# Matmul, GELU, matmul on one core: turns of `a` in halves, earlier casting loads, another order of sums, and tiles moved to multiples of 512 bytes

## Chip, core and metric

The kernel runs on one core of a Trainium2 chip. The metric is the device time of that core in microseconds, as a median of several runs.

## The reference

```python
m, k, n, p = 1024, 1024, 2048, 1024
h = a @ b                                  # a: 1024x1024, b: 1024x2048, float32
h = 0.5 * h * (1 + tanh(sqrt(2/pi) * (h + 0.044715 * h**3)))
out = h @ c                                # c: 2048x1024, float32
```

## The kernel before

The order of the work is written out by hand: every engine runs its instructions in the order in which the Python text issues them, and the tiles wait for each other through semaphores. Slots in SBUF and banks in PSUM are named by hand too (`slot`, `bank`, `pieces`), and allocated one after the other along a partition.

**Front.** `a` comes in eight loads of 512 KB (`load_a(h, q)`: half `h` of the rows, quarter `q` of the columns), and the first quarter of the columns of `b` in four (`load_b(q)`), all on SP's queue in the order a(0,0), b(0), a(1,0), then a(0,q), b(q), a(1,q) for q = 1, 2, 3. They land as float32. `cast_a` casts one load of `a` to bfloat16 on VectorE or ScalarE; `turn` transposes it on TensorE with eight 128x128 transposes into one PSUM bank, and two VectorE copies bring it to `aT`. `cast_b` casts `b` on ScalarE. `block(h, tiles, ks)` then issues matmuls of the first 512 columns of `b` against `aT`, for half `h` of the rows of `a`: 64 matmuls of 128x128 by 512 in all, four output tiles per half. Since only seven banks are free beside the bank of the turns, the fourth tile of half 1 is made last (`mm1(ps[1, 3], ...)`, in bank 7), and the last turn, a(1,3), goes through bank 0 once `gelu` has read it. The rest of `b` and all of `c` come by casting loads on POOL's queue (1 MB read, 512 KB of bfloat16 written, each). POOL's queue holds them back with one small copy, `gate` (L82), that reads the last load but two, a(0,3), and so waits for it.

**Small round, `seven(zero, ...)`.** `seven` computes a 2x2 block product with seven block products in place of eight. Its products are called P1 (A11 by B11), P2 (A12 by B21), P5, P6, P7 (products of sums), and then `p4` and `p3`. The sums `s1` to `s4` and `t1` to `t4` are made on VectorE (`dve`, L152) in the type fp32r; P1 and P2 multiply bfloat16 tiles, the other five multiply fp32r tiles. `snap` (L278) copies a product from PSUM to SBUF on ScalarE, `plus` (L283) adds it to another product on VectorE. In the round `zero` (256 columns of `b`), each product has 2 output tiles with 4 matmuls each: 56 matmuls. Its sums `s` need the casting loads of `b`.

**Middle round, `seven(one, ...)`,** does the same for the last 1024 columns of `b`: 7 products, 4 tiles, 4 matmuls each, 112 matmuls. Every output tile of both rounds goes through GELU on ScalarE into `hT`.

**Last round, `seven(two, ...)`,** is the second matmul, `hT` by `c`: 7 products, 4 tiles, 8 matmuls each, 224 matmuls with a last P2 tile kept for the very end in two halves (L349). Its results go through `ot` buffers (four of them, tag `o`) to SP's stores.

All matmuls of `seven` are issued at one line, L194. In the program as it is built, the wide tiles `c_sb`, `hT`, `aT`, `b1`, `b2`, the four slots `x0` to `x3` and all `pieces` start 448 bytes above a multiple of 512 bytes in the partition: the small tiles ahead of them end at byte 17,856 = 34 x 512 + 448, and the wide tiles all have sizes that are multiples of 512.

Of the kernel before, what the change touches and what calls it, by code (L numbers as in the profile page):

```python
# [9 lines left out]
F32 = mybir.dt.float32  # L10
# [9 lines left out]
def kernel(ctx, tc, a, b, c, out):  # L20
    nc = tc.nc
    M, K = a.shape
    _, N = b.shape
    _, P = c.shape
    H = 512
# [8 lines left out]
    consts = ctx.enter_context(tc.tile_pool(name="consts", bufs=1))  # L34
# [8 lines left out]
    def bank(i, shape=(128, H), dt=F32, name="ps"):  # L43
        return pp.tile(list(shape), dt, name=name, tag=f"bank{i}", padded_shape=None)

    def pieces(tag, bufs, shape, dt, name):
        return small.tile(shape, dt, name=name, tag=tag, bufs=bufs)
# [5 lines left out]
    gate = consts.tile([128, 1], F32, name="gate")  # L53
    g = consts.tile([128, 1], F32, name="g")

    c_sb = keep.tile([128, NT, P], BF16, name="c_sb")
    hT = [keep.tile([128, NT, H], BF16, name=f"hT{h}") for h in range(2)]
    aT = slot("a", [128, 2, KT, H], BF16, "aT")
# [6 lines left out]
    sta = [slot(f"x{i}", [128, 2, 2, 4, 256], F32, "sta") for i in (1, 3)]  # L65

    def load_a(h, q):
        nc.sync.dma_start(out=sta[q // 2][:, h, q % 2],  # L68
                          in_=av[:, 4 * h:4 * h + 4, ds(q * 256, 256)])

    def load_b(q):
        nc.sync.dma_start(out=stb[:, 2 * q:2 * q + 2], in_=bv[:, 2 * q:2 * q + 2, 0:H])  # L72

    load_a(0, 0)
    load_b(0)
    load_a(1, 0)
# [2 lines left out]
        load_b(q)  # L79
        load_a(1, q)  # L80

    nc.gpsimd.tensor_copy(gate, sta[1][:, 0, 1, 3, 0:1])  # L82
    nc.scalar.activation(g, warm[:, 0:1], AF.Gelu_apprx_tanh)


# [2 lines left out]
    for n in range(2):  # L88
        for k in range(0, KT, 4):
            nc.gpsimd.dma_start(out=b2[:, k:k + 4, ts(n, H)],  # L90
                                in_=bv[:, k:k + 4, ds(1024 + n * H, H)])
# [9 lines left out]
    def mm1(p, t, h, ks):  # L101
        for k in ks:
            nc.tensor.matmul(p, b1[:, k, ts(t, 128)], aT[:, h, k],  # L103
                             start=(k == 0), stop=(k == KT - 1))

    def gelu(t, h, p):
        nc.scalar.activation(hT[h][:, t], p, AF.Gelu_apprx_tanh)  # L107

    ps = {(0, t): bank(t) for t in range(4)}
# [7 lines left out]
    def cast_a(h, q, *engs):  # L117

        ab = pieces("ab", 2, [128, 4, 256], BF16, "ab")
        for i, eng in enumerate(engs):  # L120
            w = 256 // len(engs)
            copy(eng, ab[:, :, ts(i, w)], sta[q // 2][:, h, q % 2][:, :, ts(i, w)])
        return ab

    def turn(h, q, i, ab):
        pt = bank(i, (128, 2, H), BF16, "pt")
        for n in range(2):
            for m in range(4):
                nc.tensor.transpose(pt[:, n, ts(m, 128)], ab[:, m, ts(n, 128)], ident)  # L129
        for n in range(2):  # L130
            nc.vector.tensor_copy(aT[:, h, 2 * q + n], pt[:, n])  # L131

    def cast_b(k, n=1):
        for i in range(n):
            r = ds(i * (H // n), H // n)
            nc.scalar.activation(b1[:, k, r], stb[:, k, r], AF.Copy)

    def block(h, tiles, ks):
        for k in ks:
            for t in tiles:  # L140
                mm1(ps[h, t], t, h, (k,))
# [56 lines left out]
    def pair(i):  # L198
        x = slot(f"x{i}", [128, 2, 4, H], F32R, "x1")
        return x[:, 0], x[:, 1]  # L200
# [8 lines left out]
    one = Seven(4, quarters(b2, 0, H), BB, [None] * 4, zero.t)  # L209

    stir(256, 256, 256, 256)
    turn(0, 0, 4, cast_a(0, 0, nc.vector))
    stir(256, 128)
    cast_b(0, 2)
    cast_b(1)
    block(0, range(4), (0, 1))
    turn(1, 0, 5, cast_a(1, 0, nc.vector))
    for t in range(3):
        ps[1, t] = bank(4 + t)
    ab = cast_a(0, 1, nc.scalar, nc.scalar)  # L220
    block(1, range(3), (0,))
    turn(0, 1, 7, ab)
    block(1, range(3), (1,))
    cast_b(2)
    cast_b(3)
    ab = cast_a(1, 1, nc.scalar, nc.scalar)
    block(0, range(4), (2,))
    zero.t[0], zero.t[1] = pair(2)
    zero.t1(2, 0)
    turn(1, 1, 7, ab)  # L230
    zero.t1(2, 1)
    block(0, range(4), (3,))
    ab = cast_a(0, 2, nc.scalar)
    cast_b(4)
    cast_b(5)
    block(1, range(3), (2,))
    turn(0, 2, 7, ab)
    block(1, range(3), (3,))
    ab = cast_a(1, 2, nc.vector)
    block(0, range(4), (4,))  # L240
    turn(1, 2, 7, ab)
    zero.t2(2, 0)
    block(0, range(4), (5,))
    ab = cast_a(0, 3, nc.scalar)
    cast_b(6)
    cast_b(7)
    block(1, range(3), (4,))
    turn(0, 3, 7, ab)
    block(1, range(3), (5,))
    ab = cast_a(1, 3, nc.scalar, nc.vector)  # L250
    zero.t[2], x11 = pair(1)
    zero.t3(2, 0)
    block(0, range(4), (6, 7))
    for t in range(4):
        gelu(t, 0, ps[0, t])
    zero.t[3], x31 = pair(3)
    zero.plain_t(2, 0)
    ps[1, 3] = bank(7)
    mm1(ps[1, 3], 3, 1, range(2))
    turn(1, 3, 0, ab)  # L260
    mm1(ps[1, 3], 3, 1, range(2, 6))
    zero.t2(2, 1)
    zero.t3(2, 1)
    block(1, range(3), (6, 7))
    mm1(ps[1, 3], 3, 1, range(6, 8))
    for t in range(4):
# [14 lines left out]
    def plus(p, st):  # L281
        ot = pieces("o", 4, [128, H], F32, "ot")
        nc.vector.tensor_tensor(out=ot, in0=p, in1=st, op=ADD)  # L283
        return ot

    def seven(w, done, between):

        (A11, A12), (A21, A22) = w.A
        (B11, B12), (B21, B22) = w.B
        J = range(w.n)  # L290
        PX = X[:w.n]
        P2, PY = (X[2:], Y[:2]) if w.n == 2 else (Y, Y)
        if w is two:
            PY = (7, 4, 5, 6)
        px = [bank(i) for i in PX]
        p1, v, u = {}, {}, {}
        for j in J:
            w.product(px[j], A11, B11, j, True)
            if w is two and j == 3:
                p1[j] = pieces("ab", 2, [128, H], F32, "p1")  # L300
                nc.scalar.activation(p1[j], px[j], AF.Copy)
            else:
                p1[j] = snap("m", px[j], "p1")
        between("P1")
        for j in J if w is not two else range(3):
            p = bank(P2[j])
            w.product(p, A12, B21, j, True)
            done(0, 0, j, plus(p, p1[j]))
        between("P2")
        py = [bank(i) for i in PY]  # L310
        for j in J:
            w.product(py[j], w.s[0], w.t[0], j, True)
        between("P5")
        for j in J:
            w.product(px[j], w.s[1], w.t[1], j, False)
            v[j] = snap("v", px[j], "v")
        between("P6")
        c22 = []
        for j in J:
            w.product(px[j], w.s[2], w.t[2], j, False)  # L320
            u[j] = snap("m", px[j], "u")
            c22.append(plus(py[j], u[j]))
            between(f"P7{j}")

        def p3(first):
            for j in J:
                if first:
                    done(1, 1, j, c22[j])
                w.product(py[j], w.last_s, w.t[3], j, False)
                done(0, 1, j, plus(py[j], v[j]))  # L330
            between("P3")

        def p4(first):
            for j in J:
                if first:
                    done(1, 1, j, c22[j])
                w.product(px[j], w.s[3], w.last_t, j, False)
                done(1, 0, j, px[j])

        for i, f in enumerate((p4, p3) if w.n == 2 else (p3, p4)):  # L340
            f(i == 0)
        if w is two:

            for i in range(2):
                r = ds(i * 256, 256)
                p = bank(PY[i])
                w.product(p, A12, B21, 3, True, i * 256, 256)
                ot = pieces("e", 2, [128, 256], F32, "ot")
                nc.vector.tensor_tensor(out=ot, in0=p[:, r], in1=p1[3][:, r], op=ADD)  # L349
                store(3, i * 256, 256, ot)  # L350
# [9 lines left out]
    def between0(n):  # L360
        if n == "P1":
            zero.plain_s()
            zero.plain_t(2, 1)
        elif n == "P2":
            zero.s3()
            zero.s4(x31[:, :, 256:])
        elif n == "P5":
            zero.t4(t4, 2)
            one.last_t = t4

    def done1(i, l, j, p):
        gelu(8 + 4 * i + j, l, p)
# [29 lines left out]
    def store(mt, q0, w, ot, eng=None):  # L402
        (eng or nc.sync).dma_start(out=out[ts(mt, 128), ds(q0, w)], in_=ot)

    def done2(i, l, j, p):
        if (i, l) == (1, 0):
            ot = pieces("o", 4, [128, H], F32, "ot")
            nc.vector.tensor_copy(ot, p)
            p = ot
        n = 2 if (i, l) == (0, 0) else 1  # L410
        for q in range(n):
            r = ds(q * (H // n), H // n)
            store(4 * i + j, l * H + q * (H // n), H // n, p[:, r])

    def between2(n):
        if n == "P1":
# [45 lines left out]
```

## Time and profile before

| What | us |
|---|---|
| median of 7 runs | 120.02 |
| lowest and highest run | 119.35, 120.15 |
| the profiled execution: its own time | 120.16 |
| the profiled execution: its span | 118.4 |

The span runs from the program's first instruction to its last; 1.76 us of the execution's time lie around it. In the profile, PE is TensorE's matmuls, PEld its weight loads (which run beside matmuls), DVE is VectorE, ACT is ScalarE, POOL is GpSimd, SP issues loads and stores; a q behind an engine is its sequencer. L194 is line 194 of the kernel above. A group is written as line, engine, operation, out<-in by tile names, shapes, xcount; behind it busy time and mean duration, or, in the timeline, start and length ahead of it and in brackets the idle time before it and who ended it. A matmul's recorded duration is longer than the pace at which matmuls follow each other, since they are pipelined: the pace is read from the starts of neighbouring rows. The granted TensorE clock was 1.00 in every stage.

### The profile page before, as it was taken

The page shows a single profiled execution, that of the slowest core. Times are in us where ns is not written, and L with a number is a line of the kernel's source. Part 1 is how long each engine was busy: PE and PEld are TensorE (multiplying, and loading weights), DVE is VectorE, ACT ScalarE, POOL GpSimd, SP SyncE. Part 2 cuts the span into 40 slices and gives each one's busy share as a digit, 9 for nine tenths or more (in the row PEclk, how much of TensorE's full clock was granted, in tenths as well). Part 3 has the DMA queues.
Part 4 walks back from the last instruction along what each step waited for, and adds up shares of the span by engine and source line. Part 5 has one row for each costly group of instructions (what it writes and reads, how often), then busy time and mean ns, then how long its engine had stood idle before and what let it go on. Part 6 is the DMA issues. An engine that isn't in the chain of part 4 may idle for free.

```text
span 118.4 us, 1469 instructions
## 1 busy us (share of the span) xinstructions
PE 112.1 (95%) x535; PEld 76.9 (65%) x540; DVE 90.5 (76%) x104; ACT 58.7 (50%) x96; POOL 11.0 (9%) x21
## 2 busy tenths in 40 slices
PE   5998899999998999999999999999999999999980
PEld 5654346544866545888887444488888888888860
DVE  0243697795996799871779999999999986964670
ACT  5046756899766689246779446900042992000000
POOL 2000007952222100000000000000000000000000
PEclk9999999999999999999999999999999999999999
DMA  2999999999999999999000000061000002004993
GB/s 85 285 368 366 365 354 312 178 208 207 206 206 213 210 212 212 210 212 202 13 0 0 0 6 0 0 211 55 0 0 0 0 0 92 2 35 176 362 353 138
DMA packets 13542, 17.91 MB, mean 151 GB/s; under 512 B 736, under 2 KB 8928, under 8 KB 13536
## 3 DMA queue, kind: packets, MB, share of 16 engines
q0 software_dynamic: 5344, 7.34, 35.2%
q1 hardware_dynamic: 8192, 10.49, 26.0%
q8 instruction: 4, 0.07, 0.3%
q14 instruction: 2, 0.02, 0.0%
HBM read 20.97 MB, written 4.19 MB: 213 GB/s over the span
## 4 chain that ended last, share of the span: by engine, by line
PE 78%; DMA 8%; DVE 5%; ACT 3%; SPq 2%; issue 1%; ACTq 0%
PE ps L194 68%; PE ps L103 8%; DMA sta<-in_a_dram 8%; DVE x L152 4%; PE pt L129 2%; SPq L68 1%; DVE ot L283 1%; ACT ab L97 1%; SPq L72 1%; ACT x L184 1%; ACT x L190 1%; ACT p L278 1%; DVE ot L349 0%; ACTq L97 0%
## 5 line engine op out<-in xcount | busy, mean ns | idle before, releaser
L194 PE MATMUL ps<-x,s 128*128 128x512 f32 x128 | 29.6, 391 | 0.0
L194 PEld LDWEIGHTS ps<-x,s 128*128 128x128 f32 x128 | 24.0, 188 | 5.1
L194 PE MATMUL ps<-x,x 128*128 128x512 f32 x96 | 22.8, 393 | 0.0
L194 PEld LDWEIGHTS ps<-x,x 128*128 128x128 f32 x96 | 18.0, 188 | 4.0 <-issue 0.2
L103 PE MATMUL ps<-aT,b 128*128 128x512 bf16 x62 | 15.0, 379 | 0.7 <-DVE aT L131 0.5
L278 ACT ACTIVATE v<-ps 128x512 f32<-128x512 f32 x10 | 6.0, 599 | 17.6 <-PE ps L194 17.5
L194 PE MATMUL ps<-c_sb,hT 128*128 128x512 bf16 (+1 forms) x70 | 14.1, 355 | 0.1
L194 PE MATMUL ps<-x 128*128 128x512 f32 x56 | 13.6, 394 | 0.3 <-DVE x L152 0.3
L107 ACT ACTIVATE hT<-ot 128x512 bf16<-128x512 f32 x18 | 10.7, 625 | 3.8 <-DVE ot L283 3.7
L194 PEld LDWEIGHTS ps<-x 128*128 128x128 f32 x56 | 10.2, 188 | 3.4 <-DVE x L152 0.8
L283 DVE TENSOR_TENSOR ot<-ps,v 128x512 f32<-128x512 f32 x10 | 6.7, 688 | 6.3 <-DMA out_dram<-ot 3.9
L194 PEld LDWEIGHTS <-hT 128*128 128x128 bf16 x72 | 6.9, 98 | 7.1 <-issue 0.5
L194 PE MATMUL ps<-aT,b 128*128 128x512 bf16 x47 | 10.8, 379 | 0.1
L283 DVE TENSOR_TENSOR ot<-ps,u 128x512 f32<-128x512 f32 x10 | 6.7, 690 | 5.1 <-ACT u L278 5.1
L103 PEld LDWEIGHTS <-b 128*128 128x128 bf16 x64 | 5.8, 97 | 6.9 <-DVE aT L131 1.0
L131 DVE COPY aT<-pt 128x512 bf16<-128x512 bf16 x16 | 6.1, 420 | 5.2 <-PE pt L129 5.2
L152 DVE TENSOR_TENSOR x<-c_sb 128x1024 fp32r<-128x1024 bf16 x8 | 9.2, 1218 | 0.0
L194 PEld LDWEIGHTS <-b 128*128 128x128 bf16 x48 | 4.5, 98 | 5.9 <-DMA b<-in_b_dram 0.4
L152 DVE TENSOR_TENSOR x<-b 128x1024 fp32r<-128x1024 bf16 (+1 forms) x4 | 7.0, 1752 | 1.3 <-ACT p L278 1.3
L107 ACT ACTIVATE hT<-ps 128x512 bf16<-128x512 f32 x14 | 7.3, 595 | 0.5 <-PE ps L103 0.5
L278 ACT ACTIVATE u<-ps 128x512 f32<-128x512 f32 x10 | 5.9, 598 | 3.3 <-PE ps L194 3.2
L97 ACT ACTIVATE ab<-sta 128x512 bf16<-128x512 f32 (+1 forms) x7 | 5.0, 747 | 4.9 <-DMA sta<-in_a_dram 2.9
(39 smaller groups left out, 111.7 us busy)
## 6 DMA issues: line engine op xcount, KB each, us to landing
sta<-in_a_dram SPq DMA_DIRECT2D x8, 512.0 KB, 9.1
c_sb<-in_c_dram POOLq DMA_DIRECT2D x8, 512.0 KB, 19.7
b<-in_b_dram POOLq DMA_DIRECT2D x6, 512.0 KB, 11.2
out_dram<-ot SPq DMA_DIRECT2D x12, 256.0 KB, 2.1
stb<-in_b_dram SPq DMA_DIRECT2D x4, 512.0 KB, 8.7
out_dram<-ot SPq DMA_DIRECT2D x8, 128.0 KB, 2.0
```

Of the source, the lines that this page charges most:

```text
L68: nc.sync.dma_start(out=sta[q // 2][:, h, q % 2], in_=av[:, 4 * h:4 * h + 4, ds(q * 256, 256)])
L72: nc.sync.dma_start(out=stb[:, 2 * q:2 * q + 2], in_=bv[:, 2 * q:2 * q + 2, 0:H])
L97: nc.scalar.activation(dst, src, AF.Copy)
L103: nc.tensor.matmul(p, b1[:, k, ts(t, 128)], aT[:, h, k], start=(k == 0), stop=(k == KT - 1))
L107: nc.scalar.activation(hT[h][:, t], p, AF.Gelu_apprx_tanh)
L129: nc.tensor.transpose(pt[:, n, ts(m, 128)], ab[:, m, ts(n, 128)], ident)
L131: nc.vector.tensor_copy(aT[:, h, 2 * q + n], pt[:, n])
L152: nc.vector.tensor_tensor(out=dst[:, r], in0=x[:, r], in1=y[:, r], op=op)
L184: nc.scalar.activation(self.t[3][:, r], self.B[1][1][:, r], AF.Copy)
L194: nc.tensor.matmul(p[:, ds(c0, w)], l[:, k, ts(j, 128)], r[:, k, ds(c0, w)], start=(start and k == 0), stop=(k == self.kt - 1), skip_group ...
L278: nc.scalar.activation(st, p, AF.Copy)
L283: nc.vector.tensor_tensor(out=ot, in0=p, in1=st, op=ADD)
```

## The change

- **Addresses.** A tile `room` of 64 bytes is allocated behind the small tiles. In the built program every wide tile then starts 64 bytes later, at a multiple of 512 bytes (`c_sb` at 17,920 = 35 x 512).
- **Three small loads.** ACT's queue issues three loads of 12, 8 and 4 rows of 2 KB of `b` into a tile `lag` that nothing reads, ahead of ScalarE's table load.
- **Gate.** The small copy that holds back the casting loads reads a(1,2) in place of a(0,3), which is one load sooner in SP's order.
- **Turns.** `turn` becomes a generator: four transposes and one copy, then what the caller puts in between, then the other four and their copy. Three matmuls (once two, once one) stand between the halves, and for a(1,1) and a(1,2) one matmul of the second column step is put ahead of the turn.
- **Casts.** Every `cast_a` but the first is two instructions, one for each 128-column slice that a half turn reads; for half 1 of the rows, VectorE casts the first slice and ScalarE the second (for the last load the other way round).
- **Sums.** `t1` is made in four parts of 512 elements in place of two of 1024, `t2` starts later, and in the small round the second part of `t3`, `s3`, both parts of `t4` and then `s4` follow `s2` at once, while the two additions of P2 move behind the first of the last two products.
- **Stores.** The stores of the first output quarter of the last round go out whole and no longer as two halves.

```diff
+    consts.tile([128, 16], F32, name="room")
...
+    lag = pieces("o", 4, [128, H], F32, "lag")
+    for n in (12, 8, 4):
+        nc.scalar.dma_start(out=lag[8 * n:9 * n], in_=b[0:n, 0:H])
...
-    nc.gpsimd.tensor_copy(gate, sta[1][:, 0, 1, 3, 0:1])
+    nc.gpsimd.tensor_copy(gate, sta[1][:, 1, 0, 3, 0:1])
...
     def turn(h, q, i, ab):
         pt = bank(i, (128, 2, H), BF16, "pt")
         for n in range(2):
             for m in range(4):
                 nc.tensor.transpose(pt[:, n, ts(m, 128)], ab[:, m, ts(n, 128)], ident)
-        for n in range(2):
             nc.vector.tensor_copy(aT[:, h, 2 * q + n], pt[:, n])
+            yield
...
-    block(0, range(4), (0, 1))
-    turn(1, 0, 5, cast_a(1, 0, nc.vector))
+    ab = cast_a(1, 0, nc.vector, nc.scalar)
+    block(0, range(4), (0,))
+    block(0, range(2), (1,))
+    tn = turn(1, 0, 7, ab)
+    next(tn)
+    block(0, range(2, 4), (1,))
+    next(tn)
...
-    block(0, range(4), (4,))
-    turn(1, 2, 7, ab)
-    zero.t2(2, 0)
-    block(0, range(4), (5,))
-    ab = cast_a(0, 3, nc.scalar)
+    ab = cast_a(1, 2, nc.vector, nc.scalar)
+    block(0, range(4), (4,))
+    block(0, range(1), (5,))
+    tn = turn(1, 2, 7, ab)
+    next(tn)
+    block(0, range(1, 4), (5,))
+    next(tn)
+    zero.t1(4, 2)
+    ab = cast_a(0, 3, nc.scalar, nc.scalar)
+    block(1, range(3), (4,))
+    tn = turn(0, 3, 7, ab)
+    next(tn)
+    block(1, range(3), (5,))
+    next(tn)
...
     block(0, range(4), (6, 7))
+    zero.t2(2, 0)
     for t in range(4):
         gelu(t, 0, ps[0, t])
+    ps[1, 3] = bank(7)
+    mm1(ps[1, 3], 3, 1, range(2))
+    tn = turn(1, 3, 0, ab)
+    next(tn)
+    mm1(ps[1, 3], 3, 1, range(2, 5))
+    next(tn)
+    mm1(ps[1, 3], 3, 1, (5,))
...
-            done(0, 0, j, plus(p, p1[j]))
+            if w.n == 2:
+                p2.append(p)
+            else:
+                done(0, 0, j, plus(p, p1[j]))
...
             f(i == 0)
+            if i == 0:
+                for j, p in enumerate(p2):
+                    done(0, 0, j, plus(p, p1[j]))
...
         elif n == "P2":
+            zero.t3(2, 1)
             zero.s3()
-            zero.s4(x31[:, :, 256:])
-        elif n == "P5":
             zero.t4(t4, 2)
             one.last_t = t4
+            zero.s4(x31[:, :, 256:])
...
-        n = 2 if (i, l) == (0, 0) else 1
-        for q in range(n):
-            r = ds(q * (H // n), H // n)
-            store(4 * i + j, l * H + q * (H // n), H // n, p[:, r])
+        store(4 * i + j, l * H, H, p)
```

More of the change, by code (lines that the diff above doesn't have):

```diff
@@ L211 @@
     stir(256, 256, 256, 256)
-    turn(0, 0, 4, cast_a(0, 0, nc.vector))
+    for _ in turn(0, 0, 4, cast_a(0, 0, nc.vector)):
+        pass
     stir(256, 128)
@@ L215 @@
     cast_b(1)
-    block(0, range(4), (0, 1))
-    turn(1, 0, 5, cast_a(1, 0, nc.vector))
+    ab = cast_a(1, 0, nc.vector, nc.scalar)
[5 more added lines that the diff above has]
+    next(tn)
     for t in range(3):
         ps[1, t] = bank(4 + t)
+    zero.t[0], zero.t[1] = pair(2)
+    zero.t1(4, 0)
     ab = cast_a(0, 1, nc.scalar, nc.scalar)
     block(1, range(3), (0,))
-    turn(0, 1, 7, ab)
+    tn = turn(0, 1, 7, ab)
@@ L223 @@
+    next(tn)
     block(1, range(3), (1,))
+    next(tn)
     cast_b(2)
     cast_b(3)
-    ab = cast_a(1, 1, nc.scalar, nc.scalar)
+    ab = cast_a(1, 1, nc.vector, nc.scalar)
     block(0, range(4), (2,))
[L228 to L233, printed above, removed]
+    block(0, range(1), (3,))
+    tn = turn(1, 1, 7, ab)
+    next(tn)
+    block(0, range(1, 4), (3,))
+    next(tn)
+    zero.t1(4, 1)
@@ L234 @@
+    ab = cast_a(0, 2, nc.scalar, nc.scalar)
+    block(1, range(3), (2,))
+    tn = turn(0, 2, 7, ab)
+    next(tn)
+    block(1, range(3), (3,))
+    next(tn)
     cast_b(4)
     cast_b(5)
[L236 to L239, printed above, removed]
+    ab = cast_a(1, 2, nc.vector, nc.scalar)
     block(0, range(4), (4,))
-    turn(1, 2, 7, ab)
-    zero.t2(2, 0)
-    block(0, range(4), (5,))
-    ab = cast_a(0, 3, nc.scalar)
+    block(0, range(1), (5,))
@@ L245 @@
+    tn = turn(1, 2, 7, ab)
+    next(tn)
+    block(0, range(1, 4), (5,))
+    next(tn)
+    zero.t1(4, 2)
+    ab = cast_a(0, 3, nc.scalar, nc.scalar)
+    block(1, range(3), (4,))
+    tn = turn(0, 3, 7, ab)
+    next(tn)
+    block(1, range(3), (5,))
+    next(tn)
+    zero.t1(4, 3)
     cast_b(6)
     cast_b(7)
-    block(1, range(3), (4,))
-    turn(0, 3, 7, ab)
-    block(1, range(3), (5,))
     ab = cast_a(1, 3, nc.scalar, nc.vector)
-    zero.t[2], x11 = pair(1)
-    zero.t3(2, 0)
     block(0, range(4), (6, 7))
+    zero.t2(2, 0)
@@ L254 @@
     for t in range(4):
         gelu(t, 0, ps[0, t])
+    ps[1, 3] = bank(7)
+    mm1(ps[1, 3], 3, 1, range(2))
+    tn = turn(1, 3, 0, ab)
+    next(tn)
+    mm1(ps[1, 3], 3, 1, range(2, 5))
+    next(tn)
+    mm1(ps[1, 3], 3, 1, (5,))
+    zero.t[2], x11 = pair(1)
     zero.t[3], x31 = pair(3)
     zero.plain_t(2, 0)
[L258 to L261, printed above, removed]
+    zero.t3(2, 0)
     zero.t2(2, 1)
-    zero.t3(2, 1)
     block(1, range(3), (6, 7))
@@ L295, in seven @@
         px = [bank(i) for i in PX]
-        p1, v, u = {}, {}, {}
+        p1, v, u, p2 = {}, {}, {}, []
         for j in J:
```

## The prediction

> **What bounds the kernel now.** I read the page's totals first, then the chain of waits, then the timeline of TensorE, then the front by windows.
>
> ```profile
> PE 112.1 (95%) x535; PEld 76.9 (65%) x540; DVE 90.5 (76%) x104; ACT 58.7 (50%) x96; POOL 11.0 (9%) x21
> ```
>
> PE is busy in 95% of the span, so there is little idle time to win; what a matmul costs matters more. The chain of waits (start, length, what):
>
> ```profile
> 3.44 9.13 DMA sta<-in_a_dram
> ...
> 31.83 4.55 DVE x L152 x4
> 36.38 0.04 issue
> 36.42 3.69 PE ps L194 x15
> 40.12 0.05 issue
> 40.17 25.03 PE ps L194 x111
> ...
> 76.04 39.09 PE ps L194 x180
> ```
>
> Loads carry the first 12.6 us, VectorE's sums once in the small round (31.8 to 36.4), PE all the rest. PE's pace is read from the starts of neighbouring timeline rows:
>
> ```profile
> 23.49 2.75 PE L103 MATMUL ps<-aT,b 128*128 128x512 bf16 x12
> 26.08 3.73 PE L194 MATMUL ps<-aT,b 128*128 128x512 bf16 x16
> ...
> 98.69 7.42 PE L194 MATMUL ps<-x,x 128*128 128x512 f32 x32
> 105.94 7.42 PE L194 MATMUL ps<-x,s 128*128 128x512 f32 x32
> 113.20 1.92 PE L194 MATMUL ps<-c_sb,hT 128*128 128x256 bf16 x16
> ```
>
> bfloat16: (26.08 - 23.49) / 12 = 0.2158 us. fp32r: (105.94 - 98.69) / 32 = 0.2266, and (113.20 - 105.94) / 32 = 0.2269. An fp32r matmul of the same width takes 10.9 ns longer. Five of seven products are fp32r: 40 + 80 + 160 = 280 matmuls, so 3.05 us of the span are this difference.
>
> The front by windows (window, length, PE busy, clock, DMA share, GB/s written):
>
> ```profile
> 4.00:5.70 1.70, 1.56 (x9) 1.00 0.95 241
> 5.70:20.00 14.30, 13.15 (x92) 1.00 1.07 362
> 20.00:21.00 1.00, 0.95 (x10) 1.00 0.80 120
> 21.00:30.00 9.00, 9.00 (x49) 1.00 1.23 203
> ```
>
> The loads run at 362 GB/s, after a dip to 241 that costs 1.7 x (362 - 241) / 362 = 0.57 us, and there is a hole at 20 to 21 us, between the last plain load and the casting loads (203 GB/s written, twice that read). Who waits there:
>
> ```profile
> 18.48 0.18 POOL L82 COPY gate<-sta 128x1 f32<-128x1 f32 x1 [17.17 <-DMA sta<-in_a_dram]
> 18.60 1.62 POOL L87 DMA_DIRECT2D b<-in_b_dram  x2
> 21.32 0.63 ACT L97 ACTIVATE ab<-sta 128x512 bf16<-128x512 f32 x1 [0.34 <-DMA sta<-in_a_dram]
> 27.90 1.41 PEld L194 LDWEIGHTS <-b 128*128 128x128 bf16 x8 [0.43 <-DMA b<-in_b_dram]
> ```
>
> a(0,3) lands at 18.4, a(1,3) at 21.2 (1.4 us a load), the second casting load at 27.86. From a(1,3) to the small round (26.08) are 4.87 us, of which 1.1 are slack: its cast ends at 21.95, PE turns to it at 23.04.
>
> [...]
>
> **The change, part by part.**
>
> *Addresses.* No row of before has another address, so the effect is bounded. [...] At most the 10.9 ns go; at least nothing does (the extra may belong to the 128-column fp32r weight load, 188 ns against 98); more cost from rounder addresses has no row for it, and I allow 0.3 us. I take the whole gain, [...]. Middle round: 80 x 10.9 = -0.87. Last round up to the end of P7: 96 x 10.9 = -1.05. Behind that, 64 more would give -0.70, but DVE is close: from `t4`, which follows the end of P7 by 6.1 us, its additions and copies wait for stores to free the four `ot` buffers (2.29 and 1.58 us) and reach the last copy only 0.05 us ahead of PE's first half tile. I take -0.5. In the middle and last round DVE's sums stay ahead of PE by 0.1 us or more at the closest place (the last part of `t3`, done at 91.55, needed at 92.6, and 0.9 earlier after).
>
> *Small loads.* Three issues on ACT, some 0.5 us each (as SP's, 0.44 to 0.53), ahead of the table load (1.28): ACT is then ready at about 3.7, and its first work waits for b(0) until 6.70; free. They add 48 KB to 6.3 MB, 0.13 us, [...]. If that breaks up the dip, loads gain up to 0.57; if not, they lose 0.13. I take -0.4.
>
> *Gate one load sooner.* a(1,2) lands at about 17.0 instead of 18.4. The first casting packets follow the gate by 1.6 us (18.5 to the first bytes at 20.2), so they now start near 18.7, with 0.2 us of b(3) and 1.4 us of a(1,3) to move. [...] Nothing, if the casting queue starts slowly. I take +2.1: a(1,3) lands at 21.2 + 2.1 - 0.4 = 22.9. In return the hole goes: the second casting load lands at about 27.0 less 0.4.
>
> *Turns and casts.* Starts of PE's instructions that lie further apart than their pace add up to 2.3 us between 7.2 and 20.4, 0.68 and 0.53 the longest, at turns. Halves with three matmuls (0.65 us) between cover the 0.42 us copy, so PE's earlier work finishes near 21.5. But then a(1,3) is late next: its cast (0.63 on ACT), `gelu` of tile 0, queued behind it on ACT, whose bank 0 the turn needs (0.55), 8 transposes (8 x 0.056), 4 matmuls and 8 more (12 x 0.216), waits 0.06: 4.3 us. On DVE, `t2` (1.2) and the turn's copies stand behind the other half cast; they are through 0.1 us or more before the matmuls that read them. Small round at 22.9 + 4.3 = 27.2, that is +1.1; without the gate's part it would be about -1.5. The half casts cost ACT 10 x 0.62 for 5.2 us before, DVE 0.69 + 4 x 0.72 for 2.8, and four parts of `t1` 0.3 more: beside loads, PE waits for none of it.
>
> *Order of sums.* Before, the round takes 39.73 - 26.08 = 13.65 us for 56 matmuls (12.1 at 215.8), and PE waits 0.5 for `t4`, behind two additions (1.2), `s3` and `s4`. After, DVE does t3, s3, t4 right behind s2, so `t4` is 1.1 us earlier against s1, and s1, by the casting load, 0.9 earlier. PE no longer waits: 12.1 + 0.4 (snaps) = 12.5, -1.15. The moved additions run beside PE; GELU of those tiles is due much later.
>
> *Stores.* Three SP issues fewer at 77 to 80 us, ahead of DVE's next need of the buffers; nothing.
>
> Sum: +1.1 - 1.15 - 0.87 - 1.05 - 0.5 = -2.5 from the profiled 120.16, which is 0.14 above the median: 117.6, or **117.5** beside the runs shown.
>
> **Rivals.**
> - *Pitch stays at 226.7* (the extra is fp32r's own): the gains of 0.87, 1.05 and 0.5 and 0.44 of the small round's go, +2.86: about 120.3. [...]
> - *The casting loads crowd out a(1,3)*, the slower side. [...] With the pitch unchanged, the small round then ends at 28.5 + 12.9 = 41.4 for 39.73: 121.8. Without a faster pitch this decides from a landing at 22.5 on (22.5 + 4.3 + 12.9 = 39.7). For it: the casting queue's rate of 203 written shows that it fills the engines; against: the hole shows its slow start.
> - *Loads gain more:* aligned writes and the end of the dip bring all loads a further 0.8 forward: 116.7.
> - *The change doesn't do what it says:* halves hide copies, but loads set the front either way. In my sum this is already so.
>
> **How the numbers follow.** Pitch falls, loads as assumed or somewhat later: 0.62, 116.4 to 118.9. Loads gain more: 0.06. Pitch stays: 0.19, 119.5 to 121. Crowded out, with pitch unchanged: 0.13. A measurement of this kernel can tell about 0.3% (0.36 us) from no change. Faster: 0.62 + 0.06 + 0.06 of the third case = 0.74; same: 0.07; slower: 0.06 + 0.13 = 0.19. The range of 116.0 to 120.9 leaves out the crowded case and the best loads. The likeliest case's own range is 116.4 to 118.9.
>
> **What would show it.** Right: starts of the last round's rows of 32 fp32r matmuls 6.9 us apart; the small round 12.5 long; no wait of PE for `x` L152 in it; ACT or DVE waiting for `sta` at about 22.9; no hole at 20 to 21. Wrong: rows still 7.26 apart (then the sum fails by 2.86), or the small round starting after 28.5 or before 26.

## The result and the profile after

| | before | after |
|---|---|---|
| median of the runs, us | 120.04 (31 runs, 119.29 to 121.13) | 118.34 (12 runs, 118.11 to 120.47) |
| the profiled execution: own time, span | 120.16, 118.4 | 118.33, 116.5 |
| start of the small round | 26.08 | 25.17 |
| length of the small round | 13.65 | 12.76 |
| length of the middle round | 25.08 | 25.08 |
| last round, up to the two half tiles | 48.39 | 48.39 |

The changed kernel is faster: ratio 0.986, 95% interval 0.9837 to 0.9884. Nine of its 12 runs lie at 118.11 to 118.45 (median 118.26) and three at 119.94 to 120.47; where the runs of a kernel fall into two such groups, "lower group" below means the faster one.

The 1.8 us split in two nearly equal parts, 26.08 - 25.17 = 0.91 in the front and 13.65 - 12.76 = 0.89 in the small round. The middle and the last round are as long as before. The totals of the page give none of this away:

```profile
PE 110.6 (95%) x534; PEld 76.3 (65%) x540; DVE 90.3 (78%) x107; ACT 59.3 (51%) x99; POOL 11.0 (9%) x21
```

PE is busy for the same 95%, of a shorter span. The chain of waits now has VectorE nowhere in the small round. First its shares of the span, then pieces of it (start, length, what):

```profile
by line: PE ps L202 75.3%; PE ps L110 11.5%; PE pt L137 4.0%; DMA sta<-in_a_dram 3.3%; DVE aT L138 0.7%; PE ps L121 0.6%; DVE ab L106 0.6%; issue 0.6%; DVE ot L385 0.4%
```

```profile
0.74 3.90 DMA sta<-in_a_dram
...
25.33 2.81 PE ps L202 x13
...
28.19 11.42 PE ps L202 x49
...
39.67 23.73 PE ps L202 x105
...
74.24 39.09 PE ps L202 x180
```

From 25.33 to 113.34 only PE and its issue are left (the matmul line of `seven` is L202 now, the sums' line is L160). Loads carry the chain to 4.64 us only, where before they carried it to 12.6: the whole share of `sta` is that one piece, and behind it the front follows PE, apart from one cast and two copies of VectorE (`ab`, `aT`). The timeline of PE, as before by starts:

```profile
25.17 3.62 PE L202 MATMUL ps<-aT,b 128*128 128x512 bf16 x15
28.43 4.02 PE L202 MATMUL ps<-x,x 128*128 128x512 f32 x16
32.29 5.79 PE L202 MATMUL ps<-x 128*128 128x512 f32 x24
37.93 7.08 PE L202 MATMUL ps<-aT,b 128*128 128x512 bf16 x31
...
96.89 7.42 PE L202 MATMUL ps<-x,x 128*128 128x512 f32 x32
104.14 7.41 PE L202 MATMUL ps<-x,s 128*128 128x512 f32 x32
111.40 1.92 PE L202 MATMUL ps<-c_sb,hT 128*128 128x256 bf16 x16
```

The row at 32.29 runs through 24 matmuls where before it was broken after 10. The last rows are 104.14 - 96.89 = 7.25 and 111.40 - 104.14 = 7.26 apart, 226.6 and 226.9 ns a matmul (the record of one is 391 to 394 ns long, as they overlap): the fp32r pace is what it was. Then the front by windows (window, length, PE busy, clock, DMA share, GB/s written), first four of the changed kernel, then one of the kernel before. Behind them stand the gate, the first cast of a(1,3) and `s1`, all of the changed kernel:

```profile
4.00:5.70 1.70, 1.18 (x7) 1.00 0.89 231
5.70:19.00 13.30, 12.59 (x92) 1.00 1.07 388
19.00:20.00 1.00, 0.95 (x10) 1.00 1.22 307
20.00:21.00 1.00, 1.00 (x7) 1.00 1.22 197
```

```profile
5.70:19.00 13.30, 12.15 (x84) 1.00 1.07 363
```

```profile
16.40 0.18 POOL L89 COPY gate<-sta 128x1 f32<-128x1 f32 x1 [15.10 <-DMA sta<-in_a_dram]
20.47 0.63 ACT L104 ACTIVATE ab<-sta 128x512 bf16<-128x512 f32 x1 [0.34 <-DMA sta<-in_a_dram]
26.39 1.23 DVE L160 TENSOR_TENSOR x<-b 128x1024 fp32r<-128x1024 bf16 x1 [0.27 <-DMA b<-in_b_dram]
```

The dip at 4 to 5.7 us is still there, deeper if anything (231 GB/s for 241). The plain loads run at 388 GB/s; before, the same window from 5.7 to 19 shows 363. The hole at 20 to 21 us is closed. The gate opens at 16.40 for 18.48, yet a(1,3) is cast at 20.47 for 21.32: the casting loads did not hold it up by anything near 2 us. `s1`, which waits for a casting load, starts at 26.39 for 28.15.

### The profile page after: what moved, and what is told of

It reads as the page before. It is cut to its first block, busy times and chain, and to the rows that moved or that the text cites. A ratio compares the mean times of both kernels' runs of the same rounds, so it can differ in the third digit from the quotient of the medians.

```text
span 116.5 us, 1472 instructions
## 1 busy us (share of the span) xinstructions
PE 110.6 (95%) x534; PEld 76.3 (65%) x540; DVE 90.3 (78%) x107; ACT 59.3 (51%) x99; POOL 11.0 (9%) x21
## 4 chain that ended last, share of the span: by engine, by line
PE 91%; DMA 3%; DVE 2%; issue 1%
PE ps L202 75%; PE ps L110 11%; PE pt L137 4%; DMA sta<-in_a_dram 3%; DVE aT L138 1%; PE ps L121 1%; DVE ab L106 1%; DVE ot L385 0%
## 5 line engine op out<-in xcount | busy, mean ns | idle before, releaser
L202 PE MATMUL ps<-x,s 128*128 128x512 f32 x128 | 29.6, 391 | 0.0
L202 PEld LDWEIGHTS ps<-x,s 128*128 128x128 f32 x128 | 24.0, 188 | 5.1
L202 PE MATMUL ps<-x,x 128*128 128x512 f32 x96 | 22.9, 394 | 0.0
L202 PEld LDWEIGHTS ps<-x,x 128*128 128x128 f32 x96 | 18.0, 188 | 3.9
L110 PE MATMUL ps<-aT,b 128*128 128x512 bf16 x62 | 15.8, 379 | 0.2
L202 PE MATMUL ps<-c_sb,hT 128*128 128x512 bf16 (+1 forms) x70 | 14.1, 355 | 0.1
L202 PE MATMUL ps<-x 128*128 128x512 f32 x56 | 13.2, 392 | 0.0
L202 PEld LDWEIGHTS ps<-x 128*128 128x128 f32 x56 | 10.2, 188 | 2.6 <-ACT v L308 0.4
L202 PEld LDWEIGHTS <-hT 128*128 128x128 bf16 x72 | 6.9, 97 | 7.1 <-issue 0.5
L138 DVE COPY aT<-pt 128x512 bf16<-128x512 bf16 x16 | 6.8, 423 | 5.8 <-PE pt L137 5.8
L202 PE MATMUL ps<-aT,b 128*128 128x512 bf16 x46 | 10.6, 379 | 0.1
L160 DVE TENSOR_TENSOR x<-c_sb 128x1024 fp32r<-128x1024 bf16 x8 | 9.2, 1219 | 0.0
L137 PEld LDWEIGHTS <-ab 128*128 128x128 bf16 x64 | 4.4, 97 | 6.3 <-DVE ab L106 2.3
L202 PEld LDWEIGHTS <-b 128*128 128x128 bf16 x48 | 4.6, 98 | 5.7 <-issue 0.3
L104 ACT ACTIVATE ab<-sta 128x512 bf16<-128x512 f32 x10 | 6.0, 625 | 3.4 <-DMA sta<-in_a_dram 3.3
```

The source lines that it names most:

```text
L104: nc.scalar.activation(dst, src, AF.Copy)
L110: nc.tensor.matmul(p, b1[:, k, ts(t, 128)], aT[:, h, k], start=(k == 0), stop=(k == KT - 1))
L160: nc.vector.tensor_tensor(out=dst[:, r], in0=x[:, r], in1=y[:, r], op=op)
L202: nc.tensor.matmul(p[:, ds(c0, w)], l[:, k, ts(j, 128)], r[:, k, ds(c0, w)], start=(start and k == 0), stop=(k == self.kt - 1), skip_group ...
```

## The experiments

The theory after this reading: the tiles' addresses make the plain loads faster (front), the order of sums removes the wait in the small round, and gate, small loads and half turns are worth little. The rivals: the front's gain belongs to the small loads, the gate or the half turns; and the fp32r pace depends on an address that 64 bytes do not reach.

Five of the profiles below (small loads left out, gate back, old sums, whole turns, and 256 bytes) contain a stretch up to about 10 us in which PE runs at half pace (their first six matmuls of `block`, of 512 columns, take 333 to 427 ns each on average, where the filled turn shows 230); the last section shows it. It makes all that PE does afterwards late, so of these five only what the loads do is compared with the changed kernel, and for the old sums the length of the small round.

**The room alone, in the kernel before.**

```diff
+    consts.tile([128, 16], F32, name="room")
```

> The kernel before with only the tile room added, so that every wide tile starts at a multiple of 512 bytes. Theory A (the address makes the plain loads faster, nothing else of it does): 380 to 385 GB/s between 5.7 and 20 us for 362, a(1,3) lands near 20.4 for 21.2, the fp32r rows of the last round stay 7.25 apart, the small round starts 0.3 to 0.8 us sooner (before 26.08), the whole 0.3 to 0.9 under before. Theory B (the loads got faster because the small loads put the DMA engines out of step): no change in the rate, in the landings or in the time.

Measured: 119.0 us (11 runs, 118.43 to 119.23), ratio 0.9908 (0.9878 to 0.9939). Windows and last rows of its timeline:

```profile
5.70:19.00 13.30, 12.57 (x86) 1.00 1.07 386
```

```profile
104.75 7.41 PE L196 MATMUL ps<-x,s 128*128 128x512 f32 x32
112.00 1.92 PE L196 MATMUL ps<-c_sb,hT 128*128 128x256 bf16 x16
```

64 bytes of address alone bring 386 GB/s and 1.0 us, and leave the pace of fp32r at 7.25 per 32. Over 13.3 us the step from 363 to 386 is 13.3 x 23 / 386 = 0.79 us of loads. In the profile the small round starts 0.59 earlier (25.49). It is also 0.61 shorter (13.04), although its sums have the old order, as `s1` starts at 26.96, ahead of the 28.15 of before.

**The changed kernel without the room.**

```diff
-    consts.tile([128, 16], F32, name="room")
```

> The changed kernel without room: tiles 448 bytes above a multiple of 512 again. Theory A: the rate falls back to about 362 GB/s, a(1,3) lands 0.8 us later or more, at 21.2 or, with the casting loads beside it, later; the small round starts 0.4 to 1.0 us later than 25.17; some 0.5 to 1 us over the changed kernel. Theory B: the rate stays at 382 and the time at the changed kernel's.

Measured: lower group 119.03 (12 of 22 runs), 0.77 above the changed kernel's 118.26; the ratio over both groups is 0.9957 (0.9932 to 0.9983).

```profile
5.70:19.00 13.30, 12.16 (x84) 1.00 1.06 360
```

The rate falls back to 360, the small round starts at 25.91, and its length stays 12.76. So the addresses are 25.91 - 25.17 = 0.74 us of the front's 0.91. With the new order of sums the round is as long without the room as with it; with the old order it was not (13.65 before, 13.04 with the room).

**Two other addresses.** The room is 192 and 320 bytes, which puts the wide tiles 128 and 256 bytes above a multiple of 512. The first of the two also splits the columns of the last round's `p4` into 256 and 256 and of its `p3` into 384 and 128, to see what an fp32r matmul costs at other widths.

```diff
-    consts.tile([128, 16], F32, name="room")
+    consts.tile([128, 48], F32, name="room")
...
-                w.product(px[j], w.s[3], w.last_t, j, False)
+                for c0, wd in ((0, 256), (256, 256)) if w is two else ((0, H),):
+                    w.product(px[j], w.s[3], w.last_t, j, False, c0, wd)
```

> Two edits read in two places. (1) room is 192 bytes, so that the wide tiles start 128 bytes above a multiple of 512: if the plain loads want multiples of 128 bytes, their rate between 5.7 and 19 us is 388 GB/s as in the changed kernel; if multiples of 256 or 512, about 360. (2) In the last round the products of p4 are computed in two halves of 256 columns, those of p3 in 384 and 128, each with its own weight load. If an fp32r matmul costs a fixed 10.9 ns more than the bfloat16 pace: 120 ns for 256 columns (bfloat16: 109). [...] If its weight load of 188 ns sets the pace of narrow ones: well over 120, toward 188.

> The changed kernel with room of 320 bytes, so that the wide tiles start 256 bytes above a multiple of 512. If the plain loads want multiples of 256 bytes or of less: 388 GB/s between 5.7 and 19 us. If they want multiples of 512: about 360.

Measured, one run each: 121.56 and 120.59. The first window is that of 128 bytes, the second that of 256 bytes:

```profile
5.70:19.00 13.30, 12.38 (x89) 1.00 1.06 359
```

```profile
5.70:19.00 13.30, 12.70 (x77) 1.00 1.07 388
```

448 and 128 bytes above a multiple of 512 are slow (363, 359), 0 and 256 are fast (388, 388): of the four offsets tried, the two multiples of 256 bytes are the fast ones. The records of single DMA packets between 5.7 and 19 us show the same, so it is the packets themselves that take longer. A packet of 2 KB takes 88 ns (median) at 448 and at 128, and 84 ns at 0 and at 256; a packet of 1 KB takes 49.3 and 49.8 ns on average, and 46.1 and 46.3. The timeline of the first, in the split products:

```profile
97.78 9.30 PE L202 MATMUL ps<-x,x 128*128 128x384 f32 x64
106.92 7.89 PE L202 MATMUL ps<-x,s 128*128 128x256 f32 x64
114.64 1.92 PE L202 MATMUL ps<-c_sb,hT 128*128 128x256 bf16 x16
```

At 256 columns an fp32r matmul takes (114.64 - 106.92) / 64 = 120.6 ns. The bfloat16 matmuls of 256 columns at the end of the same trace start 109 to 110 ns apart, so the extra is about 11 ns, as at 512 columns: a fixed amount for each matmul, not a share of its columns. A time in proportion to the columns, half of 226.7 or 113.3 ns, is refuted. The row at 97.78 mixes two widths. Read one by one, its matmuls of 384 columns start 173 ns apart, which is again about 11 more than the 162.5 halfway between the bfloat16 paces at 256 and 512. Its matmuls of 128 columns start 111 ns apart, as do their weight loads: so narrow, a fixed extra no longer describes them (beside the 56 ns of a bfloat16 transpose of 128 columns, eight of which run from 17.80 to 18.25 in the kernel before, it would give 67). The address makes no difference either: 32 fp32r matmuls of 512 columns take 7.25 to 7.26 us at 448, at 0 and at 256 bytes. Where the 11 ns come from, these runs do not show. The last round is 50.74 - 48.39 = 2.35 us longer for that split, which accounts for the run's time: 121.56 - 2.35 = 119.2, near the kernel without the room.

**The three small loads left out.**

```diff
-    lag = pieces("o", 4, [128, H], F32, "lag")
-    for n in (12, 8, 4):
-        nc.scalar.dma_start(out=lag[8 * n:9 * n], in_=b[0:n, 0:H])
```

> The changed kernel without the three small loads on ACT's queue. Theory A: they do not break up the dip at 4 to 5.7 us and cost what they move; without them a(0,0) lands at 4.34 for 4.64 and b(0) at 6.7 for 6.85, later loads 0.1 to 0.2 sooner, the time the same or down to 0.3 us lower. Theory B: they put the engines out of step; without them the rate between 5.7 and 20 us falls to 362 and the time rises by 0.5 to 1 us.

Measured: lower group 118.42 (10 of 19 runs), 0.16 above the changed kernel.

```profile
4.00:5.70 1.70, 1.57 (x7) 1.00 0.90 216
5.70:19.00 13.30, 12.69 (x78) 1.00 1.06 384
```

The small loads do not make the rate, and the dip comes with and without them. That the kernel is a little slower without them, and not a little faster, neither theory says.

**The gate back on a(0,3).**

```diff
-    nc.gpsimd.tensor_copy(gate, sta[1][:, 1, 0, 3, 0:1])
+    nc.gpsimd.tensor_copy(gate, sta[1][:, 0, 1, 3, 0:1])
```

> The changed kernel with the gate on a(0,3) again. If the earlier gate is what closed the hole between plain and casting loads: hole of about 0.8 us is back, the second casting load lands at about 27.3 for 26.1, the first sum s1 starts at about 27.6 for 26.39, t4 ends 1.2 us later and PE waits for it, small round 0.6 to 1.2 us longer; a(1,3) lands no sooner, since the two queues hardly overlapped in the changed kernel. If the earlier casting loads slow a(1,3): it lands 0.3 us or more sooner than 20.36, and the small round starts sooner.

Measured: lower group 118.23 (10 of 17 runs), the same as the changed kernel within 0.03. The rate is 388. The hole is back in part (216 GB/s from 19 to 20 us for 307, 135 from 20 to 21 for 197) and costs no time.

```profile
17.65 0.19 POOL L89 COPY gate<-sta 128x1 f32<-128x1 f32 x1 [16.35 <-DMA sta<-in_a_dram]
```

The gate runs 1.25 us later than at 16.40, and the first casting packet in the trace starts at 19.35 for 19.10, only 0.25 later: with the early gate 2.7 us pass from the copy to the packet, with the late one 1.7 (as in before). Opening the gate while two more plain loads are under way buys 0.25 us of start. The first casting packet lies 0.6 us ahead of the last plain one with the late gate (19.35 and 19.93 here, 20.18 and 20.73 before) and 0.9 us with the early one (19.10 and 20.01): it is tied to the end of the plain loads more than to the gate. The first cast of a(1,3) starts at 20.33 here for 20.47 in the changed kernel, so by these two traces the early gate held it up by 0.14 us.

**The old order of sums in the changed kernel.** `t3`'s second part in the front, P2's additions at once, `s3` and `s4` ahead of `t4`.

```diff
-            if w.n == 2:
-                p2.append(p)
-            else:
-                done(0, 0, j, plus(p, p1[j]))
+            done(0, 0, j, plus(p, p1[j]))
...
         elif n == "P2":
-            zero.t3(2, 1)
             zero.s3()
+            zero.s4(x31[:, :, 256:])
+        elif n == "P5":
             zero.t4(t4, 2)
             one.last_t = t4
-            zero.s4(x31[:, :, 256:])
```

> The changed kernel with the old order of sums in the small round (the second part of t3 in the front, P2's additions right behind P2, s4 ahead of t4). Theory A (the order is worth what the traces show, small round 12.76 for 13.65 us): PE waits for t4 again, the round takes 13.3 to 13.7 us, the time is 0.5 to 0.9 us over the changed kernel's 118.3. Theory B (the shorter round comes from the earlier casting loads alone): the round stays at 12.8 to 13.0, the time within 0.2.

Measured: lower group 119.12 (10 of 22 runs), 0.86 above the changed kernel; the small round takes 13.57 for 12.76, and its timeline has the wait of before again:

```profile
34.43 2.80 PE L202 MATMUL ps<-x 128*128 128x512 f32 x10
37.57 3.46 PE L202 MATMUL ps<-x 128*128 128x512 f32 x14 [0.34 <-DVE x L160]
```

(37.57 - 34.43) - 10 x 0.2266 = 0.87 us, as much as the round is longer (0.81) and the time (0.86). The same reckoning for the two rows of before, at 33.31 and 36.42, gives 0.84. The bracket names 0.34 of idle PE; the start of the next row shows the whole loss, as the row ahead of the wait is recorded 2.80 us long, 0.53 more than 10 x 0.2266.

**Whole turns in the changed kernel.** Eight transposes, then both copies, and the matmuls that stood between the halves behind them.

```diff
         for n in range(2):
             for m in range(4):
                 nc.tensor.transpose(pt[:, n, ts(m, 128)], ab[:, m, ts(n, 128)], ident)
+        for n in range(2):
             nc.vector.tensor_copy(aT[:, h, 2 * q + n], pt[:, n])
-            yield
+        yield
+        yield
```

> The changed kernel with every turn whole: eight transposes, then the two copies, and the matmuls that stood between the halves behind them. Theory A (halves fill PE's gaps): gaps of 0.4 to 0.7 us at turns are back, the small round starts 0.3 to 0.9 us later than 25.17. Theory B (loads set the front either way): it starts within 0.2 us. On the first turn, which has nothing between its halves: whole, it leaves PE no gap of 0.68 us at 5.6, so executions in which PE runs at half pace up to 9.9 us (427 ns for a matmul of 512) should be rarer than in the changed kernel, where 3 of 12 took 1.8 us longer.

Measured: lower group 118.12 (5 of 6 runs, 118.06 to 118.21); the ratio over all six is 0.9839 (0.9793 to 0.9885). Halving the turns is worth nothing here. The half casts stay, and three matmuls still stand behind most of the whole turns, where they run beside the turn's copies, so this is not the order of before. Whether the small round starts within 0.2 us of 25.17 can't be read from this profile, because of the stretch at half pace.

**The room and the new order of sums together, in the kernel before.** The edit is the line of the first experiment, and the diff of the old order of sums read backwards.

> The kernel before with two parts of the change alone: the tile room, and the new order of sums in the small round (second part of t3 behind P2, t4 ahead of s4, P2's additions behind the first of the last two products). Turns, casts, gate, stores as before, no small loads. Theory A (these two are the whole gain): small round starts near 25.5, as with room alone, and takes 12.7 to 12.8 us; middle and last round 25.08 and 48.39 as always; span 116.9, time 118.2 to 118.5, the changed kernel's within 0.3. Theory B (halves, half casts and earlier gate carry 0.5 us or more of it): 118.7 or more.

Measured: lower group 118.81 (118.5, 118.5, 118.81, 118.91, 119.11; a sixth run took 121.42), ratio 0.9895 (0.9861 to 0.9929).

```profile
7.50 1.90 PE L105 MATMUL ps<-aT,b 128*128 128x512 bf16 x8 [1.17 <-ACT b L138]
...
25.93 3.62 PE L196 MATMUL ps<-aT,b 128*128 128x512 bf16 x16
29.19 4.01 PE L196 MATMUL ps<-x,x 128*128 128x512 f32 x16
33.04 5.77 PE L196 MATMUL ps<-x 128*128 128x512 f32 x24
38.65 1.69 PE L196 MATMUL ps<-aT,b 128*128 128x512 bf16 x7
```

The small round takes 12.73, as in the changed kernel, but starts at 25.93. Two of the seven edits give 120.04 - 118.81 = 1.2 us of 1.8, so the second theory's mark is met: 0.5 us or more belongs to other edits. And beside the room alone (119.0, with a round of 13.04) the order of sums adds 0.2 us, or 0.31 in the round, not the 0.86 that it costs to take it out of the changed kernel. What an edit is worth here depends on the others.

**The first turn filled.** The last three experiments put the two dummy matmuls that follow the first turn (`stir`, into a bank that nothing reads) between its halves. In the changed kernel this turn is the one with nothing between its halves. The second experiment also leaves the small loads out; the third repeats the first.

```diff
-    for _ in turn(0, 0, 4, cast_a(0, 0, nc.vector)):
-        pass
+    tn = turn(0, 0, 4, cast_a(0, 0, nc.vector))
+    next(tn)
     stir(256, 128)
+    next(tn)
```

> The changed kernel with the first turn's gap filled: the two dummy matmuls of 256 and 128 columns that followed the turn stand between its halves. Theory A (the gap of 0.68 us in the first turn keeps TensorE at half pace for some microseconds more in some executions): these executions, 1.8 us longer, become rare or vanish, and the others stay at 118.2 to 118.5. Theory B (they depend on when the execution starts, not on this gap): about a quarter to a half of the executions still take 1.8 us longer.

> As the one with the first turn's gap filled, and without the three small loads. If these only delay the first loads (a(0,0) at 4.2 for 4.64): first matmul of the front 0.3 us sooner, the small round up to 0.3 us sooner, 118.0 to 118.3. If they help against the executions at half pace or even out later loads: slower than with them by 0.2 us or more, or more executions that are 1.8 us longer.

> The changed kernel with the first turn's gap filled by the two dummy matmuls, once more, to count executions. If the gap is what keeps TensorE at half pace: none of the executions 1.8 us longer than 118.2, as in the eight seen with the gap filled. If it was chance: a quarter or more of them.

Measured: 118.19 (4 runs, ratio 0.9825, 0.9788 to 0.9861), 118.44 (4 runs, 0.9844, 0.9807 to 0.9881) and 118.24 (6 runs, 0.9859, 0.9833 to 0.9885). None of the 14 runs is a longer one; the filled turn with the small loads has 118.33 as its highest of 10. It is no faster than the changed kernel's lower group (118.26), but all 10 runs are there. Leaving out the small loads costs 0.20 to 0.25 here, near the 0.16 of before.

## Why the prediction was right, and where it was not

The time, 117.5 forecast in a range of 116.0 to 120.9, came out at 118.34. It was right as a sum and by luck: its two largest terms, the faster pace of fp32r and the late a(1,3), were both wrong by 2 us or more, in opposite directions, and cancelled. Both signs that the prediction named for its failure came true: rows of fp32r still 7.26 apart, after which by its own words the sum should have failed by 2.86, and a small round that starts before 26. In us against the profiled execution of before:

| Step | predicted | measured | shown by |
|---|---|---|---|
| pace of fp32r in middle and last round | -0.87 -1.05 -0.5 | 0, 0, 0 | both rounds 25.08 and 48.39; room alone |
| start of the small round | +1.1 | -0.91 | timeline |
| small round | -1.15 | -0.89 | timeline; old order of sums |
| sum | -2.5 | -1.8 | |

- **Addresses, pace: failed.** That the address makes the 10.9 ns was the author's estimate, and it was wrong: 32 fp32r matmuls of 512 columns take 7.25 to 7.26 us at 448, 0 and 256 bytes. The one number at one width could not tell a time in proportion to the columns from a fixed 10.9 ns more; the measurement at 256 columns (120.6 ns) could. The rival "Pitch stays" was right on the pace (226.6 and 226.9 ns after); its 120.3 was 2.0 too high because it kept the late front: the small round was to start 1.1 later and started 0.91 earlier.
- **Addresses, loads: in the text as a rival only.** "Loads gain more" had 0.06 of the chance, and its 0.8 us were to come from aligned writes and the end of the dip together. The addresses alone proved worth 0.77 to 1.04 us (without the room, room alone), through the plain loads, 363 to 388 GB/s. The profile of before holds one offset only, 448, so nothing in it could tell. The runs show 388 GB/s at 0 and at 256 bytes and 363 and 359 at 448 and at 128, with packets of 2 KB that take 84 ns and 88 ns. Why some offsets are slow was not shown.
- **Small loads, -0.4: failed.** The dip stayed, at 231 GB/s. Their worth is 0.16 to 0.25 us by the two experiments without them, which is near the spread of the runs; how they bring it stays open.
- **Gate, +2.1: failed, the other large error beside the pace.** a(1,3) was to land at 22.9; its cast began at 20.47. The step that failed is the start of the casting loads: forecast at 18.7, it came at 19.10, 2.7 us behind the gate. Since the plain loads were faster too, only 0.9 us of them were left then; 388 GB/s held up to 19 us. So how the two queues share the DMA engines can't be told from these runs, and the +2.1 was the author's estimate of how long casting loads hold up a(1,3). The bound "Nothing, if the casting queue starts slowly" was the right end. The forecast return came, the hole at 20 to 21 closed; it is worth nothing measurable.
- **Turns and casts: the wrong path.** The prediction let the landing of a(1,3) set the small round, 4.3 us behind it. (That chain without the gate's part, 21.2 - 0.4 + 4.3 = 25.1, is -1.0 and not the -1.5 that the prediction gives.) In the changed kernel a(1,3) does not set it: its first cast ends at 20.47 + 0.63 = 21.10, and PE turns to it at 22.08, about 1 us later, as before (1.1). Nor do loads set the front either way, as the fourth rival has it: the chain leaves them at 4.64, and in the profile of whole turns the time that PE lost up to 10 us is still missing at the start of the small round (26.54 for 25.17). PE sets the front now, with the waits that are left to it between 7 and 20 us. Faster loads shorten these waits, and so does the rest of the change (the figures stand below the list).
- **Order of sums, -1.15: right, mis-sized.** The wait is gone, and taking the step out costs 0.86. The prediction counted 56 matmuls at the bfloat16 pace (12.1 us); 40 of them are fp32r and keep 10.9 ns each, 0.44, so that 12.1 + 0.44 leave about 0.2 to the 12.76. The step's worth is 0.86 only in the changed kernel; beside the room alone it was 0.2.

What the experiments leave open: room and sums together give 1.2 us, the whole change 1.8. The remaining 0.6 belongs to no single edit that was taken out (gate, small loads, half turns: 0.25 at most each). The traces show where it lies, namely in the front. From the first matmul of `block` to the small round PE takes 26.08 - 7.17 = 18.91 us before and 18.39 with the room alone, 18.57 for the change without the room and 17.82 for the whole change. So the room is 0.5 to 0.75 of this stretch and the rest of the change 0.35 to 0.6, each more beside the other (one execution each). Which part of the rest does it was not tried: the half casts and the places of turns and of `t1`'s parts were not taken out alone, nor were the stores. The profile of room and sums takes 18.43, as the room alone does; its small round comes later (25.93 for 25.49) because its first matmul does (7.50 for 7.10).

## What to carry to other kernels

Look at where tiles that take large loads start in the partition: here 0 and 256 bytes above a multiple of 512 were fast (388 GB/s), and small tiles ahead of them that put them at 448 cost 6% of the load rate (363). One number at one size does not say where a cost comes from: measure a second size before giving one cause most of the chance. A sum that comes out right is no proof of its terms, so compare stage by stage. And what an edit costs when it is taken out need not be what it brings when it is put in alone.

## What was not expected of the hardware

In some executions PE stays at half its pace until about 10 us. The timeline of PE, first of the changed kernel with whole turns in such an execution, then of the filled turn:

```profile
7.81 2.77 PE L110 MATMUL ps<-aT,b 128*128 128x512 bf16 x6
10.37 0.75 PE L137 MATMUL pt<-ident,ab 128*128 128x128 bf16 x8
```

```profile
7.26 1.47 PE L110 MATMUL ps<-aT,b 128*128 128x512 bf16 x6 [0.51 <-ACT b L144]
8.64 0.40 PE L137 MATMUL pt<-ident,ab 128*128 128x128 bf16 x4
```

(10.37 - 7.81) / 6 = 427 ns for a matmul of 512 columns, against (8.64 - 7.26) / 6 = 230, the step to the transposes included. The profile shows a clock of 1.00 in both. The five profiled executions named above (small loads left out, gate back, old sums, whole turns, 256 bytes) have this stretch and belong to the longer ones of their kernels, where a kernel ran more than once; no other profile has it. For executions without a profile only the time tells. By the time, the longer ones were 3 of 12 of the changed kernel, 10 of 22 without the room, 9 of 19 without the small loads, 7 of 17 with the gate back, 12 of 22 with the old sums, 1 of 6 with whole turns, and none of 14 with the first turn filled. What sets the pace of 427 in these executions was not shown. In the changed kernel PE idles for 0.52 us before the first turn and for 0.52 us between its halves:

```profile
5.41 0.40 PE L137 MATMUL pt<-ident,ab 128*128 128x128 bf16 x4 [0.52 <-DVE ab L106]
6.33 0.38 PE L137 MATMUL pt<-ident,ab 128*128 128x128 bf16 x4 [0.52 <-DVE aT L138]
```

With the second gap filled it did not occur in 14 runs. That this gap alone tips it is not shown: whole turns have no second gap, and had it once in 6.
